# A plain float32 indexer, a search that is a thread of its own, and own banks for the last pieces of a two-layer trunk

## The chip, the cores and the metric

The kernel runs on one core of a Trainium2 chip. The metric is the device time of one execution in microseconds (us); the kernel before took 638.97 us (median of 3 runs, 638.91 to 639.08).

## The reference

Two layers over 256 positions of width 1024, in float32. Each layer normalizes x, projects it to seven groups of columns and runs two attentions side by side. Attention A (8 heads of 64) attends only to the 64 keys that an indexer picks for each query; attention B is a difference of two softmaxes (4 heads, two components of 64 each), with its own norm. Both see keys of their own and earlier chunks of 64. Then come the output projection, a gated feed-forward of width 2816, and at the very end a last norm.

```python
dots  = einsum('bqhd,bsd->bqhs', iq, ik) * 32**-0.5      # 8 indexer heads of 32, one key
score = einsum('bqhs,bqh->bqs', relu(dots), iw * 8**-0.5)
score = where(admissible, score, -inf);  _, idx = top_k(score, 64)
out_a = softmax(q . k[idx] * 64**-0.5) . v[idx]
out_b = rms_norm((softmax(q1.k1) - lam * softmax(q2.k2)) . v, g_subln) * (1 - lam_init)
x = x + concat(out_a, out_b) @ w_out
x = x + (silu(h2 @ w_gate) * (h2 @ w_up)) @ w_down       # h2 = rms_norm(x, g_ffn)
```

## The kernel before

The 256 positions are two blocks of 128 (b = 0 and 1), which sit on the partitions of the activations. A large product takes three passes in the fast float32 form (`mm3`, lines 205 to 215): weights and activations are each split into a high and a low part, and high by high, high by low and low by high are summed in PSUM. Weights stream in by SyncE's queue in chunks of up to 1 MB into three buffers (`wraw`); ACT casts a chunk's high part (`whi`, line 186) and DVE subtracts it for the low part (`wlo`, line 187), 1024 columns at a time, into six buffers each.

The groups of a layer run in the order idx, qb, kb, vb, qa, ka, va, then the output projection, the feed-forward in six strips of 512 columns, and the down projection. What belongs to the attentions is written as generators, threads that the planner `Weave` slips between the large matmuls: each `yield` gives a delay and the events that a thread waits for, and a clock of estimated costs decides which comes next. This fixes the order on PE. The order on DVE and ACT is made from it by the framework's scheduler, in which `tc.high_priority(offset=-LOWP)` puts the search (line 468) behind other work. Each engine works strictly in its own order. PSUM has eight banks, all of one pool: who asks for a ninth waits until the oldest one's readers are done.

The indexer begins in `after_proj` (line 397): rope gives `ixt` (9 times 32 columns: 8 query heads, 1 key); `ixq` and `ixk` (lines 405 to 411) repeat every head as high, high, low parts on 128 columns, so that one product of depth 128 holds all the products of parts; 9 transposes per block (`ptx`) bring them to `iqT` and `ikT`. `indexer` (line 448) takes two heads at a time into one bank (`dots`), ACT applies relu into one of two `relu` buffers, and DVE adds both heads to `score` with weights (line 464). The search takes 8 maxima eight times (lines 469 to 475), and its mask goes to attention A.

Attention B (`attn_b`, line 516): logits `lg_b` in plain float32 from two 64-row halves of the array (line 489), a negated maximum and mask on DVE (line 497), exp on ACT, the difference of the two softmaxes on DVE (`p_b`, line 530), transposes of it (`ppt_b`, line 512) at `DB[b]` us of the planner's clock after the logits were issued, and the product with v (`ob`). `subln` (line 556) squares and sums per head (`osq`, `ov`).

At the end of layer 1, block 1's last six row tiles of the down projection (`TAIL`, line 739) are taken by pieces of columns, 0 to 512, 512 to 768, 768 to 1024, the last two in halves of the same bank; after each piece a residual add (line 756) and a step of the last norm (`final`, line 762) follow.

## Time and profile before

| what | value |
|---|---|
| median of 3 runs | 638.97 us |
| profiled execution | 638.96 us, of which the span 637.1 us |
| mean granted clock of TensorE | 0.999 |
| PE busy | 626.2 us (98% of the span), 3091 matmuls |
| DVE busy | 435.5 us (68%) |
| ACT busy | 361.2 us (57%) |

The engines are PE (matmuls; its weight loads are a row of their own), DVE, ACT and POOL. Times in the views are microseconds from the start of the span. A row of the timeline has the start, the busy time of its group, the engine, the line of the kernel, the operation, output and inputs by the program's names, the shapes and a count; in brackets stands idle time ahead of it and what ended it. Matmuls are pipelined, so their busy times overlap: what one costs is the distance to the next start.

### The profile page before, as it was taken

To read this page: it belongs to the slowest core of one execution; us is meant where nothing else is said; L and a number is where in the kernel's file an instruction comes from. 1 tells how busy PE (TensorE), PEld (TensorE's weight loads), DVE (VectorE), ACT (ScalarE), POOL (GpSimd) and SP (SyncE) were. 2 spreads that over 40 slices of the span, in tenths; PEclk is the share of its full clock that TensorE was granted. 3 is DMA by queue.
4 is the path that set the end of the run, shared out by engine and by line. 5 is a ranking of instruction groups with operands and counts; after the bars stand their busy time and mean duration, and the time that the engine had idled before them with its cause. 6 is when DMAs were issued, how large, how long until landed. Compare 5 with 4: busy or idle time off the path is not lost.

```text
span 637.1 us, 8397 instructions
## 1 busy us (share of the span) xinstructions
PE 626.2 (98%) x3091; PEld 512.0 (80%) x3091; DVE 435.5 (68%) x925; ACT 361.2 (57%) x620; POOL 2.0 (0%) x12
## 2 busy tenths in 40 slices
PE   9999999999999999999999999999999999999995
PEld 5888777888888888888898787878888888888884
DVE  5999997696555456544598999876756555464445
ACT  4877587684454444433477777876744454453331
POOL 1000000000000000000000000000000000000000
PEclk9999999999999999999999999999999999999999
DMA  9854443346665556654286533323755555646511
GB/s 334 288 196 151 139 172 134 133 133 198 199 197 163 192 175 199 198 195 145 67 268 205 188 133 132 133 70 129 246 178 174 196 198 179 196 158 200 193 34 66
DMA packets 49369, 109.61 MB, mean 172 GB/s; under 512 B 1968, under 2 KB 6576, under 8 KB 49328
## 3 DMA queue, kind: packets, MB, share of 16 engines
q1 hardware_dynamic: 48320, 106.96, 50.4%
q10 hardware_dynamic: 1008, 2.12, 0.9%
q8 instruction: 24, 0.39, 0.3%
q14 instruction: 17, 0.14, 0.1%
HBM read 108.02 MB, written 1.05 MB: 171 GB/s over the span
## 4 chain that ended last, share of the span: by engine, by line
PE 81%; DVE 14%; issue 2%; DMA 2%; ACT 1%; ACTq 0%
PE dn L210 6%; PE dn L214 6%; PE dn L212 6%; PE ps_gate L210 6%; PE ps_gate L214 6%; PE ps_gate L212 6%; PE ps_up L214 6%; PE ps_up L212 6%; PE ps_up L210 6%; DVE wlo L187 4%; PE wo L210 2%; PE wo L214 2%; PE wo L212 2%; DVE topk L474 2%; PE pth L218 2%
## 5 line engine op out<-in xcount | busy, mean ns | idle before, releaser
L187 DVE TENSOR_TENSOR wlo<-wraw,whi 128x1024 fp32r<-128x1024 f32 (+1 forms) x200 | 241.3, 1213 | 138.3 <-ACT whi L186 134.3
L186 ACT CAST whi<-wraw 128x1024 fp32r<-128x1024 f32 (+1 forms) x200 | 207.1, 1044 | 147.4 <-PE dn L214 47.5
L210 PE MATMUL ps_gate<-whi,hi_ffn 128*128 128x512 f32 x160 | 64.3, 402 | 0.0
L214 PE MATMUL ps_gate<-whi,lo_ffn 128*128 128x512 f32 x160 | 62.5, 391 | 0.0
L214 PE MATMUL ps_up<-whi,lo_ffn 128*128 128x512 f32 x160 | 62.3, 389 | 0.0
L212 PE MATMUL ps_gate<-wlo,hi_ffn 128*128 128x512 f32 x160 | 62.3, 389 | 0.0
L210 PE MATMUL ps_up<-whi,hi_ffn 128*128 128x512 f32 x160 | 62.2, 389 | 0.0
L212 PE MATMUL ps_up<-wlo,hi_ffn 128*128 128x512 f32 x160 | 62.2, 389 | 0.0
L210 PE MATMUL dn<-whi,hi_ff 128*128 128x512 f32 (+1 forms) x182 | 59.9, 386 | 0.5 <-DVE x L756 0.5
L214 PE MATMUL dn<-whi,lo_ff 128*128 128x512 f32 (+1 forms) x182 | 59.2, 382 | 0.0
L212 PE MATMUL dn<-wlo,hi_ff 128*128 128x512 f32 (+1 forms) x182 | 59.2, 382 | 0.0
L214 PEld LDWEIGHTS dn<-whi,lo_ff 128*128 128x128 f32 x182 | 34.2, 188 | 6.7
L210 PEld LDWEIGHTS dn<-whi,hi_ff 128*128 128x128 f32 x182 | 33.9, 188 | 7.0 <-DVE x L756 0.7
L212 PEld LDWEIGHTS dn<-wlo,hi_ff 128*128 128x128 f32 x182 | 34.2, 188 | 6.6
L214 PEld LDWEIGHTS ps_gate<-whi,lo_ffn 128*128 128x128 f32 x160 | 30.0, 188 | 6.6
L210 PEld LDWEIGHTS ps_up<-whi,hi_ffn 128*128 128x128 f32 x160 | 30.0, 188 | 6.2
L214 PEld LDWEIGHTS ps_up<-whi,lo_ffn 128*128 128x128 f32 x160 | 30.0, 188 | 6.2
L212 PEld LDWEIGHTS ps_up<-wlo,hi_ffn 128*128 128x128 f32 x160 | 30.0, 188 | 6.2
L212 PEld LDWEIGHTS ps_gate<-wlo,hi_ffn 128*128 128x128 f32 x160 | 30.1, 188 | 5.7
L210 PEld LDWEIGHTS ps_gate<-whi,hi_ffn 128*128 128x128 f32 x160 | 30.1, 188 | 5.6
L316 ACT CAST hi_ff<-pth 128x512 fp32r<-128x512 f32 (+1 forms) x24 | 13.1, 548 | 21.1 <-PE pth L218 21.1
L317 DVE TENSOR_TENSOR lo_ff<-pth,hi_ff 128x512 fp32r<-128x512 f32 (+1 forms) x24 | 15.5, 646 | 8.8 <-ACT hi_ff L316 8.8
(346 smaller groups left out, 1081.5 us busy)
## 6 DMA issues: line engine op xcount, KB each, us to landing
wraw<-in_w_in_dram SPq DMA_DIRECT2D x24, 1024.0 KB, 5.1
wraw<-in_w_down_dram SPq DMA_DIRECT2D x22, 1024.0 KB, 5.0
wraw<-in_w_gate_dram SPq DMA_DIRECT2D x20, 1024.0 KB, 5.1
wraw<-in_w_up_dram SPq DMA_DIRECT2D x20, 1024.0 KB, 5.1
wraw<-in_w_out_dram SPq DMA_DIRECT2D x8, 1024.0 KB, 5.0
wraw<-in_w_idx_dram SPq DMA_DIRECT2D x8, 296.0 KB, 3.5
wraw<-in_w_gate_dram SPq DMA_DIRECT2D x4, 512.0 KB, 4.0
wraw<-in_w_up_dram SPq DMA_DIRECT2D x4, 512.0 KB, 5.0
```

The costliest lines, as they stand in the source:

```text
L186: nc.scalar.copy(hi, raw[c][:, s:s + step])
L187: nc.vector.tensor_tensor(lo, raw[c][:, s:s + step], hi.bitcast(F32), op=ALU.subtract)
L210: nc.tensor.matmul(ps, hi, whi, start=first, stop=False, skip_group_check=second)
L212: nc.tensor.matmul(ps, hi, wlo, start=False, stop=False, skip_group_check=second)
L214: nc.tensor.matmul(ps, lo, whi, start=False, stop=last, skip_group_check=second)
L218: nc.tensor.transpose(o, i, ident)
L316: nc.scalar.copy(hi[:, :n], pt)
L317: nc.vector.tensor_tensor(lo[:, :n], pt, hi[:, :n].bitcast(F32), op=ALU.subtract)
L474: nc.vector.match_replace(out=nxt[:, :nk], in_to_replace=m8, in_values=cur[:, :nk], imm_value=TAKEN)
```

## The change

Four edits go together.

The indexer works in plain float32. `ixt` now has 12 times 32 columns, the key four times, and there is no splitting into parts; three transposes per block give two tiles of four query heads and one tile with the key in all four row groups. The eight products of a block, 32 rows deep, are issued one after another into four banks, one for each row group; then come the relus and score steps.

The search is a thread `search`, spawned after the score, with a planner's delay per step (`DTOP`) instead of the low priority; attention A's logits wait for its event. Block 1's `ppt_b` is planned 12 instead of 10 us after its logits. `subln` sums its squares on ACT, head by head. In the last layer the second half of the last block is closed early and added to x, and the last two pieces of columns get banks of their own. Where a helper had a switch for the shared bank (`second` in `mm3`), it is gone; the lines of that are left out here.

```diff
@@ -30,8 +30,7 @@
 BIG = 1.0e30
 TAKEN = -3.0e38
 EPS = 1e-6
-LOWP = 100
-DG = 2.0
+DTOP = (4.0, 2.6, 2.8)
 DUP = 2.5
 DQB = 2.5
 DQA = 0.8
@@ -41,7 +40,7 @@
 DT = 1.8
 DROPE = 8.0
 DIX = 13.0
-DB = (8.0, 10.0)
+DB = (8.0, 12.0)
 DA = (5.0, 6.5)
 DPV = 4.0
 WARM = 9
@@ -399,30 +398,20 @@
             nc.vector.tensor_scalar(w, ps[:, 288:296], r, 8 ** -0.5, op0=ALU.mult, op1=ALU.mult)
             T["iw", b] = w
             a, c = rope_evac(ps, r, b, 9, 32, name)
-            t = pool.tile([P, 9, 32], F32, tag="hff", bufs=3, name=f"ixt{L}{b}")
-            nc.vector.tensor_tensor(t.rearrange("p h d -> p (h d)"), a[:, :288], c[:, :288], op=ALU.add)
-
-            sq = pool.tile([P, 8, 4, 32], F32R, tag=("kbT", "kaT")[b], bufs=1, name=f"ixq{L}{b}")
-            sk = pool.tile([P, 1, 4, 32], F32R, tag="ixk", bufs=2, name=f"ixk{L}{b}")
-            for st, hd, first, second in ((sq, slice(0, 8), slice(0, 4, 2), slice(1, 4, 2)),
-                                          (sk, slice(8, 9), slice(0, 2), slice(2, 4))):
-                src = t[:, hd].unsqueeze(2).to_broadcast([P, hd.stop - hd.start, 2, 32])
-                nc.scalar.copy(st[:, :, first], src)
-                nc.vector.tensor_tensor(st[:, :, second], src, st[:, :, first].bitcast(F32), op=ALU.subtract)
+            t = pool.tile([P, 12, 32], F32, tag="hff", bufs=3, name=f"ixt{L}{b}")
+            keys = [v[:, 256:288].unsqueeze(1).to_broadcast([P, 4, 32]) for v in (a, c)]
+            nc.vector.tensor_tensor(t[:, :8].rearrange("p h d -> p (h d)"), a[:, :256], c[:, :256], op=ALU.add)
+            nc.vector.tensor_tensor(t[:, 8:], keys[0], keys[1], op=ALU.add)
             yield DIX, ()
-            iq = pool.tile([P, 8, P], F32R, tag="iqT", bufs=2, name=f"iqT{L}{b}")
+
+            pt = bank(f"ptx{L}{b}").rearrange("p (k t) -> p k t", k=4)
+            for k in range(3):
+                transpose(pt[:, k], t[:, 4 * k:4 * k + 4].rearrange("p h d -> p (h d)"))
+            iq = T["iq", b] = pool.tile([P, 2, P], F32, tag="iqT", bufs=2, name=f"iqT{L}{b}")
             if b == 0:
-                T["ik"] = pool.tile([P, S], F32R, tag="ikT", bufs=1, name=f"ikT{L}")
-            flat = [v.bitcast(F32).rearrange("p h r d -> p h (r d)") for v in (sq, sk)]
-            for g in range(2):
-                pt = bank(f"ptx{L}{b}{g}").rearrange("p (k t) -> p k t", k=4)
-                for k in range(4):
-                    transpose(pt[:, k], flat[0][:, 4 * g + k])
-                nc.scalar.copy(iq[:, 4 * g:4 * g + 4], pt)
-            pt = bank(f"ptx{L}{b}2")
-            transpose(pt[:, :P], flat[1][:, 0])
-            nc.scalar.copy(T["ik"][:, b * P:(b + 1) * P], pt[:, :P])
-            T["iq", b] = iq
+                T["ik"] = pool.tile([P, S], F32, tag="ikT", bufs=1, name=f"ikT{L}")
+            nc.scalar.copy(T["ik"][:, b * P:(b + 1) * P], pt[:, 2])
+            nc.scalar.copy(iq, pt[:, :2])
         elif nm in ("va", "vb"):
             v = pool.tile([P, 512], F32, tag=nm, bufs=2, name=name)
             nc.scalar.activation(v, ps, AF.Copy, scale=r)
@@ -450,32 +439,38 @@
             yield 0, tuple(("idx", L, i) for i in range(b + 1))
             nk = (b + 1) * P
             sc = pool.tile([P, S], F32, tag="score", bufs=2, name=f"score{L}{b}")
+            banks = [bank(f"dots{L}{b}{g}").rearrange("p (i k) -> p i k", i=2) for g in range(4)]
+            for i in range(2):
+                for g in range(4):
+                    rws = slice(32 * g, 32 * g + 32)
+                    small_mm(0.054 * (b + 1), banks[g][:, i, :nk], T["iq", b][rws, i], T["ik"][rws, :nk],
+                             start=True, stop=True)
             first = True
             for g in range(4):
-                if g:
-                    yield DG, ()
-                ps = bank(f"dots{L}{b}{g}").rearrange("p (i k) -> p i k", i=2)
+                rl = pool.tile([P, 2, S], F32, tag="relu", bufs=2, name=f"relu{L}{b}{g}")
+                nc.scalar.activation(rl[:, :, :nk], banks[g][:, :, :nk], AF.Relu, scale=32 ** -0.5)
                 for i in range(2):
-                    small_mm(0.109, ps[:, i, :nk], T["iq", b][:, 2 * g + i], T["ik"][:, :nk], start=True, stop=True)
-                rl = pool.tile([P, 2, S], F32, tag="relu", bufs=2, name=f"relu{L}{b}{g}")
-                nc.scalar.activation(rl[:, :, :nk], ps[:, :, :nk], AF.Relu, scale=32 ** -0.5)
-                for i in range(2):
-                    h = 2 * g + i
+                    h = 4 * i + g
                     nc.vector.scalar_tensor_tensor(sc[:, :nk], rl[:, i, :nk], T["iw", b][:, h:h + 1],
                                                    smask[:, b, :nk] if first else sc[:, :nk],
                                                    op0=ALU.mult, op1=ALU.add)
                     first = False
-            with tc.high_priority(offset=-LOWP):
-                cur = sc
-                for it in range(TOPK // 8):
-                    m8 = small(8, f"m8_{L}{b}{it}")
-                    nc.vector.max(m8, cur[:, :nk])
-                    nxt = pool.tile([P, S], F32, tag="topk", bufs=3, name=f"topk{L}{b}{it}")
-                    nc.vector.match_replace(out=nxt[:, :nk], in_to_replace=m8, in_values=cur[:, :nk], imm_value=TAKEN)
-                    cur = nxt
-                m = pool.tile([P, S], F32, tag="amask", bufs=2, name=f"amask{L}{b}")
-                nc.vector.tensor_scalar(m[:, :nk], cur[:, :nk], 0.5 * TAKEN, -BIG, op0=ALU.is_gt, op1=ALU.mult)
-            T["mask", b] = m
+            W.spawn(search(L, b, sc, nk))
+
+    def search(L, b, cur, nk):
+
+        yield DTOP[0], () if b == 0 else (("mask", L, 0),)
+        for it in range(TOPK // 8):
+            m8 = small(8, f"m8_{L}{b}{it}")
+            nc.vector.max(m8, cur[:, :nk])
+            nxt = pool.tile([P, S], F32, tag="topk", bufs=3, name=f"topk{L}{b}{it}")
+            nc.vector.match_replace(out=nxt[:, :nk], in_to_replace=m8, in_values=cur[:, :nk], imm_value=TAKEN)
+            cur = nxt
+            yield DTOP[b + 1], ()
+        m = pool.tile([P, S], F32, tag="amask", bufs=2, name=f"amask{L}{b}")
+        nc.vector.tensor_scalar(m[:, :nk], cur[:, :nk], 0.5 * TAKEN, -BIG, op0=ALU.is_gt, op1=ALU.mult)
+        T["mask", b] = m
+        W.done(("mask", L, b), 1.0)
 
     def softmax_quad(L, b, q, k, mask, pairs, name):
 
@@ -554,10 +549,10 @@
                 W.spawn(subln(L, b, ob))
 
     def subln(L, b, ob):
-        sq = pool.tile([P, 4, P], F32, tag="silu", bufs=2, name=f"osq{L}{b}")
         v = small(4, f"ov{L}{b}")
-        nc.scalar.activation(sq, ob, AF.Square)
-        nc.vector.tensor_reduce(v, sq, axis=AX.X, op=ALU.add)
+        for h in range(4):
+            sq = pool.tile([P, P], BF16, tag="sqjunk", name=f"osq{L}{b}{h}")
+            nc.scalar.activation(sq, ob[:, h], AF.Square, accum_out=v[:, h:h + 1])
         nc.vector.tensor_scalar(v, v, 1.0 / P, EPS, op0=ALU.mult, op1=ALU.add)
         rs = rsqrt(v, 4, f"or{L}{b}")
         on = pool.tile([P, 4, P], F32, tag="hff", bufs=3, name=f"on{L}{b}")
@@ -588,7 +583,7 @@
         nq = 0
         for n, (b, qd) in enumerate(items):
             while nq < min(n + 2, len(items)):
-                yield (DQA if nq else 0.0), tuple((m, L, i) for m in ("qa", "ka") for i in range(items[nq][0] + 1))
+                yield (DQA if nq else 0.0), tuple((m, L, i) for m in ("qa", "ka") for i in range(items[nq][0] + 1)) + (("mask", L, items[nq][0]),)
                 qk(*items[nq])
                 nq += 1
             for pr in (2 * qd, 2 * qd + 1):
@@ -722,39 +717,42 @@
                     yield from group("ffn", L, (L, "both", j), 2 * n, False, after_both)
             nk = DFF // P
             halves = [(0, 512), (512, 1024)]
-
-            cuts = [list(halves) for b in range(NB)]
-            if L + 1 == DEPTH:
-                cuts[NB - 1] = [(0, 512), (512, 768), (768, 1024)]
             pd = [[bank(f"dn{L}{b}{h}") for h in range(2)] for b in range(NB)]
-
-            def piece(b, a, e):
-                return pd[b][a // 512][:, a % 512:a % 512 + e - a]
-
-            def down(b, cols, kt):
+            TAIL = 6
+
+            def down(b, cols, kt, banks, first, last):
                 w = parts[plan[L, "down", kt], kt]
-                mm3([(piece(b, a, e), w[0][:, a:e], w[1][:, a:e]) for a, e in cols], ffT, (L, b, kt),
-                    kt == 0, kt == nk - 1, cols[0][0] % 512 > 0)
-
-            TAIL = 6
+                mm3([(ps[:, :e - a], w[0][:, a:e], w[1][:, a:e]) for (a, e), ps in zip(cols, banks)], ffT, (L, b, kt),
+                    first, last)
+
+
+            ends = L + 1 == DEPTH
             for kt in range(nk - TAIL):
                 ensure(plan[L, "down", kt], 3, 2)
                 for b in range(NB):
                     yield 0, (("ff", L, kt // 4, b),)
-                    down(b, halves, kt)
+                    if ends and b == NB - 1 and kt == nk - TAIL - 1:
+                        for h in (1, 0):
+                            down(b, halves[h:h + 1], kt, pd[b][h:h + 1], False, h == 1)
+                        nc.vector.tensor_tensor(X[b][:, 512:], pd[b][1], X[b][:, 512:], op=ALU.add)
+                    else:
+                        down(b, halves, kt, pd[b], kt == 0, False)
             ensure(plan[L, "down", nk - 1], 3, 1)
             if L + 1 == DEPTH:
                 gfin = pool.tile([P, D], F32, tag="wraw", bufs=3, name="gfin")
                 nc.scalar.dma_start(gfin, g_final.partition_broadcast(P))
             for b in range(NB):
-                if L + 1 == DEPTH:
-                    fin = final(b, cuts[b], gfin)
-                for h, (a, e) in enumerate(cuts[b]):
+                pieces = [(ae, ps, False) for ae, ps in zip(halves, pd[b])]
+                if ends and b == NB - 1:
+                    pieces[1:] = [(ae, bank(f"dne{ae[0]}"), True) for ae in ((512, 768), (768, 1024))]
+                if ends:
+                    fin = final(b, [p[0] for p in pieces], gfin)
+                for h, ((a, e), ps, own) in enumerate(pieces):
                     for kt in range(nk - TAIL, nk):
                         yield 0, (("ff", L, kt // 4, b),)
-                        down(b, [(a, e)], kt)
-                    nc.vector.tensor_tensor(X[b][:, a:e], piece(b, a, e), X[b][:, a:e], op=ALU.add)
-                    if L + 1 == DEPTH:
+                        down(b, [(a, e)], kt, [ps], own and kt == nk - TAIL, kt == nk - 1)
+                    nc.vector.tensor_tensor(X[b][:, a:e], ps[:, :e - a], X[b][:, a:e], op=ALU.add)
+                    if ends:
                         next(fin)
                     else:
                         W.spawn(norm("mix", L + 1, b, h))
```

The order on PE in layer 0, where the indexer's transposes stand among the `kb` matmuls (numbers are those of tiles, `x4` counts equal rows). Before:

```order
L218 MATMUL ptx_347<-ident,ixq_227 128x128 x4
L218 MATMUL ptx_353<-ident,ixq_227 128x128 x4
L218 MATMUL ptx_359<-ident,ixk_228 128x128
L218 MATMUL ptx_363<-ident,ixq_243 128x128 x4
L218 MATMUL ptx_369<-ident,ixq_243 128x128 x4
L218 MATMUL ptx_375<-ident,ixk_244 128x128
L210 MATMUL ps_kb_308<-whi_0_275,hi_mix_142 128x512
```

After, from the second half of block 0's eight products (`dots_360` to `363` are the four banks of block 0, `389` to `392` those of block 1; each bank gets two products):

```order
L434 MATMUL dots_360<-ikT_340,iqT_339 128x128
L434 MATMUL dots_361<-ikT_340,iqT_339 128x128
L434 MATMUL dots_362<-ikT_340,iqT_339 128x128
L434 MATMUL dots_363<-ikT_340,iqT_339 128x128
L434 MATMUL dots_389<-ikT_340,iqT_347 128x256
L434 MATMUL dots_390<-ikT_340,iqT_347 128x256
L434 MATMUL dots_391<-ikT_340,iqT_347 128x256
L434 MATMUL dots_392<-ikT_340,iqT_347 128x256
```

In place of nine transposes of a block stand three, and the products, which stood in pairs between `kb` matmuls, are one run over both blocks.

The order on ACT in layer 0, where relu frees the banks. Before, with the banks `385` and `414` of block 0 and the copies of `qb` that was transposed:

```order
L186 CAST whi_2_404<-wraw_273 128x1024
L186 CAST whi_0_484<-wraw_309 128x1024
L461 ACTIVATE relu_388<-dots_385 128x2x128
L186 CAST whi_2_488<-wraw_309 128x1024
L461 ACTIVATE relu_417<-dots_414 128x2x128
L376 COPY qb00T<-ptq_qb_422 128x512
L376 COPY qb01T<-ptq_qb_429 128x512
```

After, where `372` to `384` are the relus of block 0 and `401` to `409` those of block 1:

```order
L451 ACTIVATE relu_372<-dots_360 128x2x128
L451 ACTIVATE relu_376<-dots_361 128x2x128
L451 ACTIVATE relu_380<-dots_362 128x2x128
L451 ACTIVATE relu_384<-dots_363 128x2x128
L451 ACTIVATE relu_401<-dots_389 128x512
L185 CAST whi_2_500<-wraw_299 128x1024
L451 ACTIVATE relu_405<-dots_390 128x512
L451 ACTIVATE relu_409<-dots_391 128x512
L375 COPY qb00T<-ptq_qb_437 128x512
```

The relus stand together now, ahead of one cast and of the copies of `qb`.

The order on PE in layer 0 at block 1's first `ppt_b`, behind the logits `lg_b` from which its `p_b` is made. Before:

```order
L445 MATMUL lg_b_970<-kbT_596,qb01T 128x256
L210 MATMUL ps_ka_824<-whi_0_827,hi_mix_156 128x512
L212 MATMUL ps_ka_824<-wlo_0_828,hi_mix_156 128x512
L214 MATMUL ps_ka_824<-whi_0_827,lo_mix_157 128x512
L210 MATMUL ps_ka_824<-whi_0_827,hi_mix_156 128x512
L212 MATMUL ps_ka_824<-wlo_0_828,hi_mix_156 128x512
L214 MATMUL ps_ka_824<-whi_0_827,lo_mix_157 128x512
L218 MATMUL ppt_b_1012<-ident,p_b_854 128x128 x4
L210 MATMUL ps_ka_824<-whi_2_831,hi_mix_156 128x512
```

After:

```order
L209 MATMUL ps_va_981<-whi_0_860,hi_mix_132 128x512
L211 MATMUL ps_va_981<-wlo_0_861,hi_mix_132 128x512
L213 MATMUL ps_va_981<-whi_0_860,lo_mix_133 128x512
L209 MATMUL ps_va_981<-whi_0_860,hi_mix_132 128x512
L211 MATMUL ps_va_981<-wlo_0_861,hi_mix_132 128x512
L213 MATMUL ps_va_981<-whi_0_860,lo_mix_133 128x512
L217 MATMUL ppt_b_1006<-ident,p_b_799 128x128 x4
L209 MATMUL ps_va_981<-whi_2_864,hi_mix_132 128x512
```

Six matmuls stand between the logits and `ppt_b` before, fifteen after; it has moved from the `ka` group into the `va` group.

## Rows read from the trace of the kernel before

**Rows 1.** The page, busy time of the engines (us, share of the span, instructions).
```profile
PE 626.2 (98%) x3091; PEld 512.0 (80%) x3091; DVE 435.5 (68%) x925; ACT 361.2 (57%) x620; POOL 2.0 (0%) x12
```

**Rows 2.** Waits of PE: engine line waited for: us in total, times, longest.
```profile
PE ppt_b L218 <- DVE p_b L530: 2.0, 2, 1.0
PE dn L210 <- DVE x L756: 0.5, 1, 0.5
```

**Rows 3.** Timeline of PE in layer 0: start us, us, engine, line, operation, tiles.
```profile
27.27 0.50 PE L212 MATMUL ps_kb<-wlo,hi_mix 128*128 128x512 f32 x1 [0.32 <-DVE wlo L187]
28.54 1.04 PE L218 MATMUL ptx<-ident,ixq 128*128 128x128 f32 x8
34.89 0.34 PE L445 MATMUL dots<-ikT,iqT 128*128 128x128 f32 x2
35.06 1.06 PE L218 MATMUL ptq_qb<-ident,rp_qb 128*128 128x128 f32 x8
35.88 0.48 PE L210 MATMUL ps_kb<-whi,hi_mix 128*128 128x512 f32 x1
40.73 0.73 PE L445 MATMUL dots<-ikT,iqT 128*128 128x128 f32 x4
41.29 0.40 PE L210 MATMUL ps_vb<-whi,hi_mix 128*128 128x512 f32 x1
44.02 0.40 PE L445 MATMUL dots<-ikT,iqT 128*128 128x256 f32 x2
44.25 0.40 PE L210 MATMUL ps_vb<-whi,hi_mix 128*128 128x512 f32 x1
```

**Rows 4.** Timeline of PE: float32 products of the second attention, 64 rows deep.
```profile
50.52 0.71 PE L445 MATMUL lg_b<-kbT,qb00T 64*128 64x128 f32 x8
51.17 0.51 PE L210 MATMUL ps_vb<-whi,hi_mix 128*128 128x512 f32 x1
68.65 1.14 PE L445 MATMUL lg_b<-kbT,qb01T 64*128 64x256 f32 x8
69.71 0.44 PE L218 MATMUL ppt_b<-ident,p_b 128*128 128x128 f32 x2
```

**Rows 5.** Timeline of DVE in layer 0 beside the indexer.
```profile
24.90 0.68 DVE L411 TENSOR_TENSOR ixq<-ixt,ixq 128x512 fp32r<-128x512 f32 x1
26.00 2.35 DVE L187 TENSOR_TENSOR wlo<-wraw,whi 128x1024 fp32r<-128x1024 f32 x2
33.16 1.22 DVE L187 TENSOR_TENSOR wlo<-wraw,whi 128x1024 fp32r<-128x1024 f32 x1
34.29 0.69 DVE L432 TENSOR_TENSOR rp_qb<-rp_qb,rp_qb 128x512 f32<-128x512 f32 x1
34.89 0.35 DVE L464 SCALAR_TENSOR_TENSOR score<-relu,iw,smask 128x128 f32<-128x128 f32 x1
35.16 1.22 DVE L187 TENSOR_TENSOR wlo<-wraw,whi 128x1024 fp32r<-128x1024 f32 x1
```

**Rows 6.** Timeline of ACT in layer 0: one relu.
```profile
35.26 0.38 ACT L461 ACTIVATE relu<-dots 128x256 f32<-128x256 f32 x1 [0.45 <-PE dots L445]
```

**Rows 7.** Timeline of PE around a late transpose of the second attention, layer 0.
```profile
80.67 0.40 PE L214 MATMUL ps_ka<-whi,lo_mix 128*128 128x512 f32 x1
82.05 0.83 PE L218 MATMUL ppt_b<-ident,p_b 128*128 128x128 f32 x4 [0.99 <-DVE p_b L530]
82.64 0.47 PE L210 MATMUL ps_ka<-whi,hi_mix 128*128 128x512 f32 x1
```

**Rows 8.** Timeline of DVE before that transpose.
```profile
80.05 0.67 DVE L560 TENSOR_REDUCE ov<-osq 128x4 f32<-128x512 f32 x1
```

**Rows 9.** Timeline at the end, all engines.
```profile
627.33 0.42 DVE L756 TENSOR_TENSOR x<-dn,x 128x256 f32<-128x256 f32 x1 [0.54 <-PE dn L214]
627.80 0.39 PE L210 MATMUL dn<-whi,hi_ff 128*128 128x256 f32 x1 [0.52 <-DVE x L756]
630.74 0.41 DVE L756 TENSOR_TENSOR x<-dn,x 128x256 f32<-128x256 f32 x1
```

8 lines of the change are left out of this document (4 added, 4 removed).

## Prediction

> **What bounds the kernel now.** I read the page's busy times first: PE is busy for 98% of the span, DVE for 68%, ACT for 57% [rows 1]. So a change pays where it takes matmul time from PE, or a wait of PE for another engine; time saved on DVE or ACT pays only through such a wait. Next I read the list of PE's waits: two stand in it that this change touches, `ppt_b` waiting for DVE (twice, 1.0 us each) and `dn` waiting for the last residual add (0.5 us) [rows 2]. Then I went along PE's timeline from one start to the next, because the printed durations of pipelined matmuls overlap: twelve 512-column matmuls take 2.73 us from 41.29 to 44.02 [rows 3], 0.227 each. DVE's timeline [rows 5] shows no idle mark beside the indexer of layer 0: each row starts where the one before ends, so in that stretch anything that PE wants from DVE is as late as DVE's queue is long. The profiled execution took 638.96 us (span 637.1), the median is 638.97, so I add the terms to 639.0.
>
> **Transposes.** 36 (18 per layer) become 12. Eight take 0.82 us from 35.06 to 35.88 [rows 3], 0.103 each; 24 fewer give 2.47 us, 1.24 per layer. All stood on PE (the first at 28.54 [rows 3]), and what ACT copies out afterwards gets smaller.
>
> **Dot products.** Before, a pair of 128 columns costs 0.17 us (34.89 to 35.06) and a pair of 256 costs 0.23 (44.02 to 44.25) [rows 3]; four pairs of each are 1.60 per layer, and up to 0.05 more in each full matmul behind a pair, say 1.85. After, they are plain float32, 32 rows deep, in four row groups and four banks. No row shows that. The nearest are the float32 products of the second attention, 64 deep in two row groups: a set of four takes 0.65 us at 128 columns (50.52 to 51.17) and 1.06 at 256 (68.65 to 69.71) [rows 4]. Twice the columns add 0.41, so a set is 0.24 fixed and 0.41 per 128 columns for two rounds of two products. If four groups run together, a block's eight products are again two rounds: 0.65 for block 0 and 1.06 for block 1, with 0.11 for the full matmul behind, 1.82 per layer, against 1.85: nothing gained, nothing lost. If only two run together, as rows 4 show, it is 1.06 + 1.88 + 0.11 = 3.05, 1.2 more per layer. If none do, 1.88 + 3.52 + 0.11 = 5.5, 3.7 more. I take four together, since groups do share in rows 4: the four products have eight records (x8) in 0.41 us, 0.051 each, where a 128-column transpose needs 0.103, so two records run at a time, one of each group.
>
> The rows show sharing by two only. The Trainium skill, "TensorE: Matmul & The Clock Gate", Part 3 (packing small matmuls), says that tiles in different row groups run concurrently, and gives a measured speedup of 3.07 rather than 4 for four row tiles of 32 rows; no run here shows it. By that figure a layer's dots would be 0.4 us dearer than mine, and the forecast 636.1.
>
> **Layer 0's new bank waits: the term against the change.** The eight banks now hold four of block 0 and four of block 1 at once, the blocks' products standing directly behind each other, with two `ps_kb` banks beside them. So block 1's last two products wait for the relus of block 0's first two banks, and the two `ptq_qb` transposes behind them need the banks of `relu` 2 and 3. There are two relu buffers: relu 2 starts when both score steps of relu 0 are done on DVE, relu 3 after both of relu 1, and DVE is the engine without slack. I walk DVE through its new order. A split (`wlo`) takes 1.13 (33.16 to 34.29), a 512-column add or multiply 0.60 (34.29 to 34.89), a score step 0.27 (34.89 to 35.16) or its own 0.35 where the next one needs it [rows 5]. By the first two lengths an operation is 0.07 and 1.04 ns per column, so the 288-column rope add is 0.37 and its successor, 256 and 128 columns, 0.54. The stretch from 24.90 to 26.00 (ixq, ixk, that add) becomes 0.54 alone, and starts 0.17 late through block 0's own split add: 25.07 to 25.61. Three splits end at 29.0, five rope steps at 32.0, a split at 33.15, an add at 33.75, a score step at 34.0, a split at 35.15, the second score step at 35.5; a relu is 0.38 [rows 6], so `ptq_qb` of block 0 can start at 35.9. The next split ends at 36.55, two score steps at 37.25, the relu at 37.65, so `ptq_qb` of block 1 starts then and ends at 38.05. In the kernel before, both end at 35.88 [rows 3]. From there to the `vb` group both kernels have the same 18 matmuls and the two small lambda products; before it takes 5.41 us, to 41.29 [rows 3], with two dots pairs and more inside. Without the pair of 128 columns (0.22 with what follows) up to 40.73, and the four products at 40.73 (0.56), it is 4.63, so the new kernel begins `vb` at 42.7; the old one has three pairs of 0.23 still to do, which makes it 42.0 for equal work. Layer 0's indexer thus loses 0.7 us, although its transposes save 1.24 and the split that PE waits for at 27.27 [rows 3] now comes in time. The waits in it are about 2 us; if DVE is no brake they are nothing.
>
> In layer 1 the products of the two blocks are kept apart by nine matmuls and the transposes, and block 1's `ptq_qb` has 12 more ahead of it. DVE reaches its first score step there earlier than before, since twice the 1.10 of 24.90 to 26.00 becomes 0.54 [rows 5], and those nine matmuls and block 1's transposes are over 2 us more for DVE than it has in layer 0. So I count no wait (the worst would be layer 0's 2 us again), and the saving of 1.24 plus 0.03 stands.
>
> **The waits that should go.** At 82.05 `ppt_b` of block 1 starts 1.38 us after the matmul at 80.67, of which 0.23 is that matmul; its four transposes take 0.59 to 82.64 where half of eight is 0.41 [rows 7]. Lost: 1.15 + 0.18 = 1.33. The list of waits has two of a kind [rows 2], one per layer, 2.66 in all. The new order puts nine matmuls more, 2.04 us, ahead of it. Each wait is shorter than that, and DVE gets there earlier besides: the reduction of 0.58 at 80.05 [rows 8] goes, and ixq and ixk before it (the delay of 0.7 in layer 0 moves PE, so it helps here). I take both waits as gone; the lower bound is nothing gained.
>
> **The rest.** ACT loses casts and gets four short squares instead of one, DVE loses more than it gets, the search keeps its operations and changes only places on DVE: nothing, beside a PE that is never short of them for long. If the search, no longer of low priority, delays a split that PE is due to use, the price is about 0.5 us a time (a maximum and a match of 128 columns, estimated as two score steps of 0.27 [rows 5]). At the end the own bank takes away PE's wait of 0.52 at 627.80, but the last residual add starts only at 630.74, behind a dense row of DVE work that begins with the add at 627.33 [rows 9]. The same work stands ahead of it in the new order, apart from one step of 0.07. I take 0.07, between 0 and 0.5.
>
> **Sum.** Layer 0: +0.7 - 1.33 = -0.63. Layer 1: -1.24 - 0.03 - 1.33 = -2.60. End: -0.07. In all -3.3: 635.7 us.
>
> **Rivals.**
> 1. The bank waits of layer 0 don't bind, because DVE meets its score steps earlier than I walked it. Then layer 0 gains 1.24, the 0.32 at 27.27 [rows 3] and 1.33, 2.9 instead of 0.63: 633.4. For it: the walk hangs on five rope steps being ready in time and no order of priorities shifting; against it: each step is a row.
> 2. Row groups share by two only. Layer 1 pays 1.2; in layer 0 the longer products lie inside the wait for relu 2 and cost nothing: 636.9.
> 3. The `ppt_b` waits stay, because the search's steps, now interleaved earlier, take the place that the ixq and reduction left on DVE: 638.3, not to be told from no change. Against it: the 2.04 us that PE now has ahead of them.
> 4. Slower: the row groups don't share at all with four banks open. Layer 1 pays 3.7. In layer 0 `ptq_qb` would be reached only at about 38.3, past relu 3, and ends 1.1 later than I have it. Together -3.3 + 4.8: 640.5. It decides against the change from about 4.6 us of extra dots time; rows 4 speak against it.
>
> **Chances.** Forecast 0.46 (its own range 634.4 to 636.8), rival 1 0.16, rival 2 0.14, rival 3 0.13, rival 4 0.06, and 0.05 for a loss that I don't see, counted as slower. A measurement can't tell 0.2% (1.3 us) from no change, so faster is below 637.7: nearly all of the forecast and of rivals 1 and 2, 0.73 after some taken off for mixtures; same 0.15, slower 0.12. The range goes from 632.8, past rival 1, to 638.7, past rival 3.
>
> **What would show it.** Right: `dots` of block 0 as eight products in some 0.65 us; in layer 0 a wait of PE at `ptq_qb` for relu, twice, about 1 us each, and `vb` beginning near 42.7; no wait of `ppt_b` for `p_b` in either layer; layer 1's indexer about 1.3 us shorter; the last residual add still ending a dense DVE chain near 3.4 us after the first. Wrong: dots of block 0 at 1.06 (rival 2) or 1.9 (rival 4); `ptq_qb` without a wait (rival 1); `ppt_b` in the list of waits (rival 3).

## The result and the profile after

The changed kernel takes 647.70 us (646.74 to 648.60), the kernel before on the same chip 639.03 (638.91 to 639.18): a ratio of 1.0135 [1.0116, 1.0154]. The forecast of 635.7 with its range to 638.7 missed, in its sign too. The profiled execution has a span of 646.8 us, 9.7 more than before. Of the four executions two take 646.7 and 646.9 at a mean granted clock of 0.996, the other two, the profiled one among them, 648.5 and 648.6 at 0.991. The page shows PE busier than in [rows 1] by 2.1 us, although its indexer transposes need 2.58 us less by their steps; DVE has the same work, ACT less:

```profile
PE 628.3 (97%) x3099; PEld 510.1 (79%) x3099; DVE 435.9 (67%) x918; ACT 356.7 (55%) x636; POOL 1.9 (0%) x12
```

The waits of PE (as in [rows 2]): both `ppt_b` waits of 1.0 and that of `dn` are gone, as forecast, and others have come, of which the longest are these:

```profile
PE ppt_b L217 <- DVE p_b L525: 2.9, 1, 2.9
PE wo L209 <- ACT hi_mb L318: 2.1, 2, 1.0
PE po L434 <- ACT pT_a L508: 1.4, 2, 0.7
PE dots L434 <- ACT relu L451: 1.3, 1, 1.3
...
```

Some names first. `on` is attention B's output after its norm, `pt_mb` its transposes, and `hi_mb` and `lo_mb` the high and low parts made from them, which the output projection `wo` multiplies. Attention A's logits are `lg_a`, `mx_a` and `pT_a` belong to its softmax, `po` is its product with v, `hi_ma` and `lo_ma` the parts of its output. `kaT` holds A's transposed keys. A name with `rp_` belongs to rope, and `relu` feeds the indexer's score. `gate` is the first product of the feed-forward.

To place the loss I took PE's first start at each landmark in both traces (us):

| PE reaches | before | after | difference |
|---|---|---|---|
| `vb` group, layer 0 | 41.29 | 44.04 | +2.75 |
| first logits `lg_a`, layer 0 | 93.30 | 93.31 | +0.01 |
| `gate` group, layer 0 | 132.62 | 137.15 | +4.53 |
| `qb` group, layer 1 | 326.43 | 330.95 | +4.52 |
| `kb` group, layer 1 | 338.25 | 342.11 | +3.86 |
| `vb` group, layer 1 | 352.35 | 356.47 | +4.12 |
| `qa` group, layer 1 | 366.64 | 370.42 | +3.78 |
| first `lg_a`, layer 1 | 404.77 | 410.10 | +5.33 |
| `gate` group, layer 1 | 443.66 | 453.69 | +10.03 |
| its last matmul | 629.94 | 639.19 | +9.25 |

So there are three places: the indexer of layer 0, attention B of layer 1, and, in both layers, the stretch from `lg_a` to the feed-forward, +4.52 and +4.70, of which the prediction has nothing. The first `lg_a` is no mark of equal work, though: behind it the changed kernel still has four `ppt_b`, four `ptq_ka` and three `va` matmuls that lay ahead of it before, about 1.5 us by their steps at full clock. So some 3 us of each stretch are loss, and layer 0's indexer is not made good at 93.31, where PE seems to be level.

**Layer 0's indexer.** PE's timeline, all records of `dots` first, block 1's last twelve in the second row:

```profile
31.15 1.15 PE L434 MATMUL dots<-ikT,iqT 32*128 32x128 f32 x20
33.58 1.45 PE L434 MATMUL dots<-ikT,iqT 32*128 32x256 f32 x12 [1.28 <-ACT relu L451]
34.96 0.80 PE L209 MATMUL ps_kb<-whi,hi_mix 128*128 128x512 f32 x1
35.55 0.63 PE L211 MATMUL ps_kb<-wlo,hi_mix 128*128 128x512 f32 x1
...
38.11 0.45 PE L211 MATMUL ps_kb<-wlo,hi_mix 128*128 128x512 f32 x1
```

ACT at that time; the relu that PE needs is behind a cast which waits for its weights, relus 2 and 3 (the last two rows) behind score steps on DVE:

```profile
32.20 1.04 ACT L185 CAST whi<-wraw 128x1024 fp32r<-128x1024 f32 x1 [1.25 <-DMA wraw<-in_w_in_dram]
33.15 0.65 ACT L451 ACTIVATE relu<-dots 128x256 f32<-128x256 f32 x2
35.80 0.38 ACT L451 ACTIVATE relu<-dots 128x256 f32<-128x256 f32 x1 [2.00 <-DVE score L454]
37.58 0.38 ACT L451 ACTIVATE relu<-dots 128x256 f32<-128x256 f32 x1 [1.40 <-DVE score L454]
```

Stretches of 2 us (length, PE's busy time and count, granted clock of TensorE, DMA share, GB/s):

```profile
32.00:34.00 2.00, 0.72 (x9) 1.00 1.03 386
34.00:36.00 2.00, 2.00 (x15) 0.70 0.04 14
36.00:38.00 2.00, 2.00 (x6) 0.50 0.63 153
```

The bank wait of the prediction is there, one step earlier (at `dots`, not at `ptq_qb`). Both blocks' products take 3.81 us (31.15 to 34.96), 2.07 more than the 0.66 and 1.08 they take in layer 1 (rows further down), where nothing is waited for. And the wait has a tail: behind it the granted clock is 0.50, the lower of TensorE's two levels (1.2 of 2.4 GHz), and six 512-column matmuls take 2.56 (35.55 to 38.11), 0.43 each instead of 0.227. With the slow one ahead of them (34.96 to 35.55) that is about 1.5 us more.

**Attention B of layer 1.** PE waits 2.89 us for the first `ppt_b` and has half clock behind it, for eight matmuls at 0.43:

```profile
379.05 0.59 PE L217 MATMUL ppt_b<-ident,p_b 128*128 128x128 f32 x2 [2.89 <-DVE p_b L525]
379.39 0.64 PE L209 MATMUL ps_qa<-whi,hi_mix 128*128 128x512 f32 x1
379.83 0.63 PE L211 MATMUL ps_qa<-wlo,hi_mix 128*128 128x512 f32 x1
...
```

What DVE does before it. Work of the search's maxima (`m`) from the start of `kb` to the first difference of softmaxes, before and after:

```profile
338.25:368.45 30.20, 5.16 (x24) 1.00 0.52 171
```
```profile
342.11:378.64 36.53, 12.43 (x48) 1.00 0.40 132
```

The rows count maxima together with the value loads and replacements that they feed: 24 are eight search steps, 48 are all sixteen, the searches of both blocks. `wlo` has ten instead of eight there. In layer 0 of the changed kernel only ten of the sixteen steps stand ahead of the first `p_b`, and no `ppt_b` waits for one. DVE's timeline shows them interleaved with the softmax, step for step:

```profile
365.50 0.42 DVE L465 MAX8 m<-score 128x8 f32<-128x256 f32 x1
...
371.44 0.28 DVE L492 CUSTOM_DVE_ANT_0 p_b<-lg_b,smask 128x128 f32<-128x128 f32 x1
...
376.25 0.41 DVE L465 MAX8 m<-topk 128x8 f32<-128x256 f32 x1
...
378.64 0.61 DVE L525 SCALAR_TENSOR_TENSOR p_b<-p_b,rc_b,p_b 128x128 f32<-128x128 f32 x2
```

The second search starts at 365.50, just before the logits `lg_b` are made (366.15 on PE). Nothing holds it until they are done.

**The end of the attentions.** PE in layer 0, before:

```profile
105.04 1.13 PE L445 MATMUL lg_a<-kaT,qa01T 64*128 64x256 f32 x8
106.60 0.60 PE L218 MATMUL pt_mb<-ident,on 128*128 128x128 f32 x4
...
108.52 1.13 PE L445 MATMUL lg_a<-kaT,qa01T 64*128 64x256 f32 x8
109.58 1.09 PE L445 MATMUL po<-pT_a,va 128*64 128x128 f32 x16
```

and after:

```profile
105.23 1.13 PE L434 MATMUL lg_a<-kaT,qa01T 64*128 64x256 f32 x8
...
108.26 1.31 PE L434 MATMUL lg_a<-kaT,qa01T 64*128 64x256 f32 x8
110.02 0.66 PE L434 MATMUL po<-pT_a,va 128*64 128x128 f32 x8 [0.46 <-DVE mx_a L492]
111.40 0.93 PE L434 MATMUL po<-pT_a,va 128*64 128x128 f32 x8 [0.72 <-ACT pT_a L508]
...
113.75 0.60 PE L217 MATMUL pt_mb<-ident,on 128*128 128x128 f32 x4
115.83 0.73 PE L209 MATMUL wo<-whi,hi_mb 128*128 128x512 f32 x2 [1.04 <-ACT hi_mb L318]
```

The last product `ob` of block 1 is late (102.64; before 97.41), with it the norm of attention B: `pt_mb` comes 7 us later, and the norm's root, a chain of small steps, now stands on DVE among the last row maxima of attention A's softmax, from

```profile
105.99 0.17 DVE L556 TENSOR_SCALAR ov<-ov 128x4 f32<-128x4 f32 x1 [0.37 <-ACT osq L555]
...
109.21 0.40 DVE L492 CUSTOM_DVE_ANT_0 p_a<-lg_a,amask 128x256 f32<-128x256 f32 x1
```

PE has matmuls of the output projection for that time, but too few: it waits 2.22 us in the three rows above.

### The profile page after: what moved, and what is told of

Read it like the earlier page. It is cut to its first block, busy times and chain, and to the rows that moved or that the text cites. A ratio compares the mean times of both kernels' runs of the same rounds, so it can differ in the third digit from the quotient of the medians.

```text
span 646.8 us, 8420 instructions
## 1 busy us (share of the span) xinstructions
PE 628.3 (97%) x3099; PEld 510.1 (79%) x3099; DVE 435.9 (67%) x918; ACT 356.7 (55%) x636; POOL 1.9 (0%) x12
## 3 DMA queue, kind: packets, MB, share of 16 engines
HBM read 108.02 MB, written 1.05 MB: 169 GB/s over the span
## 4 chain that ended last, share of the span: by engine, by line
PE 64%; DVE 21%; ACT 9%; issue 4%; DMA 2%; DVEq 0%; ACTq 0%
DVE wlo L186 7%; PE ps_gate L209 6%; PE ps_gate L213 6%; PE ps_gate L211 6%; PE ps_up L213 6%; PE ps_up L211 6%; PE ps_up L209 6%; PE dn L213 5%; PE dn L211 5%; PE dn L209 5%; ACT p_a L495 2%; DVE score L454 2%; PE wo L209 2%; DVE topk L467 2%; PE wo L213 2%
## 5 line engine op out<-in xcount | busy, mean ns | idle before, releaser
L209 PE MATMUL dn<-whi,hi_ff 128*128 128x512 f32 x170 | 56.6, 393 | 0.0
L213 PE MATMUL dn<-whi,lo_ff 128*128 128x512 f32 x170 | 56.0, 390 | 0.0
L211 PE MATMUL dn<-wlo,hi_ff 128*128 128x512 f32 x170 | 55.9, 389 | 0.0
L213 PEld LDWEIGHTS dn<-whi,lo_ff 128*128 128x128 f32 x170 | 31.9, 188 | 6.7
L211 PEld LDWEIGHTS dn<-wlo,hi_ff 128*128 128x128 f32 x170 | 31.9, 188 | 6.6
L209 PEld LDWEIGHTS dn<-whi,hi_ff 128*128 128x128 f32 x170 | 31.6, 188 | 6.3
L495 ACT ACTIVATE p_b<-p_b,mx_b 128x128 f32<-128x128 f32 (+1 forms) x32 | 14.3, 448 | 13.4 <-DVE mx_b L492 13.3
```

The lines of the kernel that those rows point to most:

```text
L209: nc.tensor.matmul(ps, hi, whi, start=first, stop=False)
L211: nc.tensor.matmul(ps, hi, wlo, start=False, stop=False)
L213: nc.tensor.matmul(ps, lo, whi, start=False, stop=last)
L495: nc.scalar.activation(p[:, i, :nk], p[:, i, :nk], AF.Exp, scale=-1.0, bias=mx[:, i:i + 1], accum_out=sm[:, i:i + 1])
```

## The experiments

Each was timed against the kernel before on its chip (638.9 to 639.0). "After" is the changed kernel. Edits are given without the lines that only pass a name.

**The delay of `ppt_b` taken back.**

```diff
-DB = (8.0, 12.0)
+DB = (8.0, 10.0)
```


> The changed kernel with block 1's ppt_b planned 10 us after its logits again instead of 12; everything else as changed. Theory D (the later ppt_b moves block 1's last ob and so its subln into the last softmaxes of attention A, and that is where the 4.5 us per layer between the first logits of attention A and the feed-forward are lost): most of that goes, some 3 us per layer, and the two waits of ppt_b of 1.3 us come back at worst: 640 to 644 us. Rival U (the squares of subln on ACT make that loss) or rival S (the search's new place on DVE does): the loss stays 4 to 5 us per layer and the ppt_b waits come back, 647 to 650.

647.66 us, 1.0139 [1.0119, 1.0159]: no change from after. PE still reaches layer 0's `gate` 4.85 late, and the old waits of `ppt_b` don't come back; `lg_a` waits 1.9 us for `kaT` instead. The delay is not what keeps the loss up in this kernel.

**The old search** (the steps back in the indexer at low priority, logits of A no longer waiting for its event), alone and with the old delay:

```diff
-            W.spawn(search(L, b, sc, nk))
+            with tc.high_priority(offset=-LOWP):
+                ... (the search before)
```


> The changed kernel with the search written behind the scores at low priority again, and attention A's logits not waiting for its event. Theory D: only layer 1's wait of 2.9 us at the first ppt_b and the half clock behind it (1.6 us) go, since the search's steps no longer stand ahead of p_b on DVE: 642 to 644 us, with the loss at the end of the attentions unchanged at about 4.5 us per layer. Rival S (the search's place on DVE makes both losses): 636 to 639. Rival U: as theory D.

> The changed kernel with both taken back: block 1's ppt_b at 10 us and the search at low priority behind the scores. Theory D: both gains add, 635 to 640 us. Rival U: the loss at the end of the attentions stays, 643 to 646.

650.12, 1.0176 [1.0160, 1.0191], and 649.14, 1.0156 [1.0139, 1.0173]. Both are slower than every theory had them; `ppt_b` waits 4.6 us in three places in the first. So it isn't the new form of the search: at low priority all sixteen steps are also ahead of layer 1's first `p_b` on DVE.

**The old sum of squares in `subln`.**

```diff
-        for h in range(4):
-            nc.scalar.activation(sq, ob[:, h], AF.Square, accum_out=v[:, h:h + 1])
+        nc.scalar.activation(sq, ob, AF.Square)
+        nc.vector.tensor_reduce(v, sq, axis=AX.X, op=ALU.add)
```


> The changed kernel with subln's squares in one ACT instruction and the sums on DVE again. Theory D: 646 to 648 us, since the chain behind the squares (the reciprocal root on DVE) is as long as before and begins as late. Rival U (the four squares with their sums delay the exps on ACT and the root on DVE): 638 to 641.

649.57, 1.0166 [1.0151, 1.0181]. ACT's squares are not the cause: without them it is 1.9 slower still, above both ranges.

**The indexer, out of after and into before** (the part of `after_proj` and the `dots` loop exchanged as a whole).

> The changed kernel with the indexer of before (parts, 18 transposes and paired products per layer); search thread, block 1's ppt_b at 12 us, subln and tail as changed. Theory X (the loss comes with the new indexer: all eight scores of a block become ready in one bunch, and DVE's order then takes them, the searches and more splits ahead of attention B's softmaxes): 636 to 640 us, and no wait of ppt_b in layer 1. Rival R (the other three edits make the loss together, none of them alone): 645 to 650.

> The kernel before with the new indexer alone (12 transposes, products in four row groups); search, delays, subln and tail of before. Theory X: 647 to 651 us, with the wait of ppt_b in layer 1 of about 3 us and the waits at the end of both attentions. Rival R: 636 to 639.

After with the old indexer takes 642.08 (640.62 to 643.96), 1.0050 [1.0034, 1.0065]: 5.6 of the 8.7 us are gone, and with them all but 0.2 of the wait of `ppt_b`. That lies between what the two theories gave. What is left stands at the end of layer 1's attentions, where `wo` waits 2.2 us for `hi_mb`: the other edits cost something there without the new indexer. Before with the new indexer takes 648.41, 1.0148 [1.0131, 1.0165], with these waits:

```profile
PE ppt_b L218 <- DVE p_b L521: 5.6, 3, 3.1
PE wo L210 <- ACT hi_mb L319: 2.4, 2, 1.2
```

The indexer alone brings the loss, though it has less work on PE. Here fourteen of the sixteen steps stand ahead of the first `p_b` of layer 0 as well, and its first `ppt_b` waits too, 2.22 and 0.26. What it changes for the others is when scores are ready: in layer 1 block 1's last score step starts 15.4 us after the start of `kb` (357.52), before 24.1 (362.37). That DVE's order, made from readiness, therefore takes both searches first is so far an inference, which the next run tests.

**The search held.** If that is the cause, holding the search by a dependency must give the time back. Its first maximum has to overwrite a copy of the reciprocal sums of block 0's first (search of block 0) or second (search of block 1) difference of softmaxes in attention B, with an event for the planner:

```diff
+HOLD = (0, 1)
...
-        yield DTOP[0], () if b == 0 else (("mask", L, 0),)
+        yield DTOP[0], (("qkb", L, HOLD[b]),) if b == 0 else (("mask", L, 0), ("qkb", L, HOLD[b]))
...
+            if it == 0:
+                nc.vector.tensor_copy(m8[:, 0:2], T["rcb", HOLD[b]])
             nc.vector.max(m8, cur[:, :nk])
...
+            T["rcb", 2 * b + hp] = r1
+            W.done(("qkb", L, 2 * b + hp), 0.0)
```


> The changed kernel with each block's search made to begin with a copy of a value that attention B's softmax gives (the reciprocal sums of its first, for block 1 its second pair of heads), so that on DVE no search step can stand ahead of them; the copied value is overwritten and not used. Theory X, the part on the search: layer 1's wait of 3 us at the first ppt_b and the half clock behind it go, 4 to 5 us; if the waits at the end of the attentions come from attention B being late, they go as well: 636 to 643 us. Rival P (products, banks and PE's shorter path make the loss, the search only fills DVE): 646 to 650.

639.00 (637.98 to 640.79), 1.0000 [0.9990, 1.0009]: all 8.7 us are back, with one small copy more per block. From PE's waits `p_b` is gone, and so are `po` and `wo`:

```profile
PE dots L435 <- ACT relu L452: 1.3, 1, 1.3
...
PE ppt_b L218 <- DVE mx_a L495: 0.8, 2, 0.4
...
```

It does two things at once, though: the mask's later event also moves attention A's last logits on PE.

```profile
107.68 1.13 PE L435 MATMUL lg_a<-kaT,qa01T 64*128 64x256 f32 x8
109.24 0.60 PE L218 MATMUL pt_mb<-ident,on 128*128 128x128 f32 x4
109.77 1.13 PE L435 MATMUL lg_a<-kaT,qa01T 64*128 64x256 f32 x8
110.83 1.09 PE L435 MATMUL po<-pT_a,va 128*64 128x128 f32 x16
```

`pt_mb` stands between the two sets again, as before, and nothing waits there.

The two additional splits (`wlo`) ahead of `p_b` explain little of it. In e7 ten stand between the start of layer 1's `kb` and the first `p_b` as well (12.06 us of DVE), with 0.80 us of `m`, and `p_b` comes 31.08 us behind it: before 30.20, in the changed kernel 36.53.

**The place on PE alone.** After, with block 1's mask event 12 us later for the planner; DVE's order ahead of `p_b` stays, with all sixteen steps in layer 1.

```diff
-        W.done(("mask", L, b), 1.0)
+        W.done(("mask", L, b), 12.0 if b else 1.0)
```


> The changed kernel, with the planner told that block 1's mask is done 12 us after its search is planned instead of 1. DVE's order ahead of attention B's softmaxes stays as changed (all 16 search steps of layer 1 before the first p_b); only PE's order moves: attention A's logits of block 1 come 12 matmuls of the output projection later, as in the run with the search held back. Theory X with two parts (the waits at the end of the attentions, 2.6 us per layer, come from those logits standing too early on PE; the 3 us wait and the half clock in layer 1 from the search on DVE): the first go, 4 to 5.5 us, the second stay: 642 to 644 us. Rival Y (the search on DVE alone makes both): 646.5 to 649. Rival Z (PE's order alone makes both): 638 to 640.

644.59 (643.09 to 645.68), 1.0086 [1.0071, 1.0102], 3.1 less than after and 0.6 above what two parts were expected to leave. Layer 0's `gate` comes 1.49 late instead of 4.53, with `pt_mb` between the logits; of these 3.04 us 1.06 are there at `vb` already, since in this execution no slow clock follows the relu wait. The searches' place stays as dear as it was in layer 1:

```profile
PE ppt_b L217 <- DVE p_b L525: 2.9, 1, 2.9
PE wo L209 <- ACT hi_mb L318: 1.6, 1, 1.6
```

So the loss has both parts: the order on DVE ahead of `p_b`, and the place of A's last logits on PE. Which part rules differs by layer. From the start of `vb` to the start of `gate`, where these three kernels have the same work (before has six dots products more there, 0.7 us), PE's time against before is (us, profiled executions):

| | after | e9, logits moved | e7, search held too |
|---|---|---|---|
| layer 0 | +1.78 | -0.20 | -0.72 |
| layer 1 | +5.91 | +5.99 | -0.88 |

In layer 0 the logits' place gives back 2.0 of the 2.5 us. In layer 1 it gives back nothing while the searches stand ahead of `p_b`, though four more slow matmuls behind that wait in e9 (0.8 us) hide a part.

**Before with the delay of 12 alone.** The waits that the prediction counts as 2.66 us, taken away in the old kernel.

```diff
-DB = (8.0, 10.0)
+DB = (8.0, 12.0)
```


> The kernel before with block 1's ppt_b planned at 12 us instead of 10, nothing else. By the prediction's step: both waits of 1.3 us go, 636.2 to 637. Rival: they go, but block 1's last ob and its subln come later and are waited for at the end of the attentions, as in the changed kernel: 638.5 to 643.

647.45 (645.98 to 648.39), 1.0130 [1.0116, 1.0144]: 8.5 us slower, more than even the rival gave. PE is 1.79 us ahead at layer 0's `va`, so the gain exists; then

```profile
112.29 0.73 PE L210 MATMUL wo<-whi,hi_mb 128*128 128x512 f32 x2 [2.50 <-ACT hi_mb L319]
...
114.72 1.05 PE L210 MATMUL wo<-whi,hi_mb 128*128 128x512 f32 x2
115.58 1.05 PE L212 MATMUL wo<-wlo,hi_mb 128*128 128x512 f32 x2
```

Two matmuls take 0.86 (114.72 to 115.58) instead of 0.45: half clock. PE reaches `gate` 3.48 late in layer 0, 9.45 in layer 1. A transpose that comes later without a wait brings its product, its norm and its column of the output projection later too, and PE has no other work left then. Late alone is not the price: in e7 block 1's `ob` comes at 102.36, in the changed kernel at 102.64, and there no `hi_mb` is waited for.

**Before with the search held**, the control for e7:

> A control: the kernel before, with its indexer, and the search as a thread held back by the copied value. Theory X (holding the search back repairs what the new indexer broke; with the old indexer it stood behind attention B's first softmaxes for the most part anyway): 637 to 640 us. Rival H (holding the search back is worth several us by itself, and the new indexer's loss is only covered by it): 630 to 635.

651.52, 1.0197 [1.0179, 1.0215], against both theories. A's logits of block 1 begin at 114.24 there (before 105.04), behind all matmuls that could have filled the time: over both layers `hi_ma` is then waited for 2.2 us and `lo_ma` 1.7, and `on`, ahead of the logits, 2.5. Holding is no gain in itself; it must put the logits neither too early (after) nor too late (this).

**The held kernel's limits**: the old delay of `ppt_b`, and holding one softmax longer, each on top of e7.

```diff
-DB = (8.0, 12.0)
+DB = (8.0, 10.0)
```


> The run with the search held back, with block 1's ppt_b planned at 10 us again instead of 12. If the two waits of ppt_b in layers 0 and 1 (1.3 us each in the kernel before) go for the reason of the prediction, by the 2 us of delay, they come back: 1 to 3 us longer than the run with the search held back alone, 640 to 642. If they went because DVE has less ahead of p_b, the time stays within 0.7 us of it.

```diff
-HOLD = (0, 1)
+HOLD = (1, 2)
```


> As the run with the search held back, one pair of heads later for both blocks (block 0 behind the second softmax of attention B's block 0, block 1 behind the first of its block 1). Theory X: nothing more to win at attention B, which no longer waits; attention A's masks come later and may be waited for: 638 to 641 us. If attention B is still the late one, 636 to 638.

643.17, 1.0067 [1.0052, 1.0082], and 642.40, 1.0057 [1.0040, 1.0074]: 3.4 to 4.2 us worse than e7 and outside what was expected, with `lg_a` waiting for `kaT` (2.2 and 1.7) and `pt_mb` for `on`. In the first `ppt_b` doesn't wait for `p_b` again: with the searches held, 10 would have been late enough for that. That 12 is still better there must have another reason, probably the place of all that follows; no run takes it apart.

**Layer 0's relu wait**, on top of e7: block 1's `dots` 6 us of the planner's clock later in both layers (e8), 2 us in layer 0 (e13), four relu buffers instead of two (e14), both of the last (e16).

```diff
-            yield 0, tuple(("idx", L, i) for i in range(b + 1))
+            yield (2.0 if b and L == 0 else 0), tuple(("idx", L, i) for i in range(b + 1))
...
-                rl = pool.tile([P, 2, S], F32, tag="relu", bufs=2, name=f"relu{L}{b}{g}")
+                rl = pool.tile([P, 2, S], F32, tag="relu", bufs=4, name=f"relu{L}{b}{g}")
```


> As the run with the search held back, and block 1's products planned 6 us behind block 0's, so that they don't meet in the eight banks in layer 0. Theory X: layer 0's wait for relu of 1.3 us and the half clock behind it of 1.6 us go too, 2 to 3 us less than the run with the search held back alone. Rival W (the relu wait is given back later, since DVE is the engine without slack there): the same time as that run, within 0.7 us.

> The run with the search held back, and in layer 0 alone block 1's products 12 matmuls behind block 0's; the order at the end of the attentions is unchanged. If layer 0's wait for relu (1.3 us at the products, 0.3 to 0.5 at ptq_qb, and a half clock in some executions) is lost time of its own: 1.3 to 2 us less than the run with the search held back, 637 to 637.7, faster than before. If DVE sets the end of that stage: within 0.6 us of it.

> The run with the search held back, with four relu buffers instead of two, so that relu 2 and 3 don't wait for the score steps. The wait at the products (the first relu stands on ACT behind a cast that waits for its weights) stays, the one at ptq_qb goes: 0.3 to 0.6 us less at most, 638.4 to 638.8; if DVE sets the end of the stage: no change within 0.3.

> Both: the products apart in layer 0 and four relu buffers, with the search held back. If the waits in layer 0 are lost time: the sum of both gains, 636.5 to 637.5; if DVE sets the end of the stage: as the run with the search held back, 638.4 to 639.4.

| run | us | ratio | what PE waits for |
|---|---|---|---|
| e8 | 640.06 | 1.0017 [1.0008, 1.0027] | no relu; `rp_ka` 1.2, `mx_a` 1.0 later on |
| e13 | 640.13 | 1.0016 [1.0007, 1.0025] | relu, now at `ptq_qb`: 2.9 in two |
| e14 | 639.23 | 1.0002 [0.9993, 1.0011] | relu 0 behind its cast: 1.9 |
| e16 | 636.57 | 0.9961 [0.9948, 0.9973] | no relu |

Two waits stand in a row: the banks wait for relu 0 and 1 (behind the cast that waits for weights), `ptq_qb` for relu 2 and 3 (behind the two buffers). Each edit takes one away and PE stands at the other. In e8, which takes both away by the longer delay, other waits come. e8 and e13 are both slower than either of their theories gave. With both edits, PE goes through:

```profile
34.42 1.15 PE L435 MATMUL dots<-ikT,iqT 32*128 32x256 f32 x16
35.50 1.09 PE L218 MATMUL ptq_qb<-ident,rp_qb 128*128 128x128 f32 x8
```

e16 (636.33 to 636.61) beats both kernels: 2.4 us below before, 11.1 below after, with all of the change's edits in it, and inside its expectation.

## Why the prediction was wrong

**Right.** The transposes: PE spends 2.58 us less on `ptx` over both layers (3.69 to 1.11), by its steps from one start to the next; 2.47 was forecast. The dots: block 0's eight products take 0.66 (344.38 to 345.04), block 1's 1.08 (347.57 to 348.65), where 0.65 and 1.06 were forecast; rivals 2 and 4 are out. In e8, where `dots` wait for nothing, all of them cost 3.45, before 3.60.

```profile
344.38 0.73 PE L434 MATMUL dots<-ikT,iqT 32*128 32x128 f32 x16
345.04 0.55 PE L217 MATMUL ptx<-ident,ixt 128*128 128x128 f32 x3
...
347.57 1.15 PE L434 MATMUL dots<-ikT,iqT 32*128 32x256 f32 x16
348.65 0.66 PE L217 MATMUL ptq_qb<-ident,rp_qb 128*128 128x128 f32 x4
```

The Trainium skill, "TensorE: Matmul & The Clock Gate", Part 3 (packing small matmuls), gives a speedup of 3.07 for four row tiles of 32 rows at 512 columns; by it they would have been 0.4 dearer per layer, an estimate. These rows, at 128 and 256 columns, show the price of full sharing.

Layer 1's indexer: from `qb` to `qa` PE gains 0.74, which would be 1.05 without a new wait of 0.31 for `rp_kb`; 1.27 was forecast.

The tail: no wait of `dn`, and the last residual add 3.04 behind the first (637.35 to 640.39) instead of 3.41; 0.4, inside the bounds 0 to 0.5 though 0.07 was put. The two `ppt_b` waits of [rows 2] are gone.

**"the search keeps its operations and changes only places on DVE: nothing".** This step failed first. The place was the price: in layer 1 eight steps more, 7 us of maxima and replacements by the windows above (12.43 against 5.16 with their pairs), ahead of the first `p_b`. The sentence that followed allowed 0.5 us a time for a split delayed by one search step; a step takes 0.65 to 0.78 by the same windows, and sixteen of them ahead of a softmax were not asked for. Rival 3 had the mechanism, but at the price of the old waits (2.66) and in their place, block 1's `ppt_b`. The new one is block 0's, 2.89 and 1.6 more by eight matmuls at half clock, and of it the argument of 2.04 us, which counts what PE has more ahead of block 1's, says nothing. e6 shows the indexer to be enough for it, e2 and e4 that the search's new form isn't needed, and e7 that holding the search removes it.

**"I take both waits as gone", for 2.66.** They went, and the gain did not stay. The step took a later start for free because PE has other work. e15 is this term by itself: +8.5 us instead of −2.66. What is late next is `ob`, the norm and `hi_mb` at the end of the attentions, where PE's other work runs out. In the changed kernel A's last logits stand too early besides: e9 moves only them, for 3.1. The prediction has no term for where the mask's event puts them on PE.

**"Layer 0's indexer thus loses 0.7 us".** The mechanism is right, relu and banks, and so is the walk through DVE: relu 2 starts at 35.80 and relu 3 at 37.58, where 35.5 and about 37.25 were walked. Two things were missing: the first relu stands behind a cast that waits for a DMA, not behind DVE's steps; and half clock behind the wait, by which PE comes to `ptq_qb` so late (38.64) that nothing is waited for there. So rival 1's sign, `ptq_qb` without a wait, came without its reason. That the products lose 2.07, where about 2 were walked for the two waits at `ptq_qb`, is luck: it is another wait. `vb` begins at 44.04, forecast 42.7: 1.3 late, near the 1.5 of the slow matmuls. This term is in the 8.7 too. e16, which is without the wait, reaches layer 0's `gate` 1.01 ahead of before, e7 1.28 behind it.

**What stays open.** The parts don't add: the old indexer in after leaves +3.1, the new one in before gives +9.5, the delay alone +8.5, the whole +8.7. Each of them moves the orders that the others are built on, and I have no sum for that. How much of e7's gain is DVE's order and how much PE's is told only by e9's 3.1 and the remaining 5.6, and by the table of the two layers, in a kernel where the two may influence each other: no run holds the search and leaves the logits where they were.

## What to carry to other kernels

An edit that makes data ready earlier can slow a kernel down: look on each in-order engine what now stands ahead of the operation that the bottleneck waits for next. Here it was work that nobody needed yet; low priority did not hold it back (e2), a dependency did (e7). A wait that is removed by putting an operation later has to be followed to the end of its chain, to the point where the bottleneck engine has no other work left; and of two waits in a row, removing either alone gained nothing by the medians (e13 was 1.1 us slower than e7, e14 0.2), both together 2.4 us (e16).

## What the runs showed of the hardware

A wait of PE can have a price behind it that its length alone doesn't tell: after 1.28 us six 512-column matmuls took 0.43 each, after 2.89 eight, 1.5 and 1.6 us more; in e9 it was twelve after 2.88. It is not certain to come: in the profiled execution of e7 the matmuls behind a wait of 1.31 take 0.23 each, in e6 those behind one of 2.22 too (64.29), in e4 six behind one of 2.22 (64.33) are slow, and behind the two of 1.0 in before none is slow. Of e7's ten executions four have a mean clock of 0.998 and spans of 636.2 to 636.8, the others 0.991 to 0.996 and 637.2 to 639.0; e16, without that wait, stays within 0.3 us. So a part of what e16 gains is the clock: at 0.998 e7 takes 638.0 to 638.6 us, e14 637.4 and 637.5, e16 636.6.

Four row groups of 32 rows in four banks ran together at the price worked out from two groups of 64 (0.66 and 1.08 against 0.65 and 1.06). And six score steps of 128 columns that each need the one before took 0.40 apiece on DVE:

```profile
36.73 2.43 DVE L454 SCALAR_TENSOR_TENSOR score<-relu,iw,score 128x128 f32<-128x128 f32 x6
39.12 0.48 DVE L454 SCALAR_TENSOR_TENSOR score<-relu,iw,smask 128x256 f32<-128x256 f32 x1
```

In [rows 5] an instruction that needs nothing of it starts 0.27 after such a step. My walk through DVE took 0.27 and 0.35.
